# Pair DMAs behind dt's weights, an earlier split of the gated result, a state copy on VectorE and two transposes swapped, in a hybrid SSD and attention layer

## The chip, the cores and the metric

The kernel runs on one core of one Trainium2 chip. The metric is the device time in microseconds of one execution, the median over several runs; lower is better. The engines of the core are TensorE (PE in the profile, with PEld for its weight loads), VectorE (DVE), ScalarE (ACT), GpSimd (POOL) and SyncE (SP). Each engine works through its own queue in the order in which its instructions were queued. DMAs are issued from the queues of SP, ACT and POOL; in the profile's DMA tables SP's are q1, ACT's q10 and POOL's q0.

## The reference

One decoder layer (`DEPTH` 1) on 256 tokens of width 2048, in float32. Cut to what matters here:

```python
u = rmsnorm(h, norm_mix_pre)
proj = u @ w_in                       # z | x,B,C | dt | q | k | v
xbc = silu(causal_depthwise_conv(xbc, conv_w, conv_b))       # width 4
dt = softplus(dt_raw + dt_bias)                              # 32 heads
y = ssd_chunked(xh, dt, -exp(a_log), bm, cm)                 # chunks of 128 tokens
y = y + d_skip * xh
yg = y * silu(z)                                             # per group of 4 heads:
yg = yg * rsqrt(mean(yg * yg) + EPS)
y_ssm = yg * ssm_norm_w
y_att = dilated_attention(q, k, v)                           # three dilations, 16 heads
h = h + rmsnorm(concat(y_ssm, y_att) @ w_out, norm_mix_post)
h = h + rmsnorm(relu(rmsnorm(h, norm_mlp_pre) @ w_up) ** 2 @ w_down, norm_mlp_post)
```

In `ssd_chunked` the second chunk's output takes in a state that the first chunk leaves for each group: `states = B^T (decay * x dt)`, and `y_off = exp(a_cs) * (C @ state)`.

## The kernel before

**Precision and weights.** Each operand of a product is split into a high and a low part (`split`, lines 144 to 150): ScalarE writes the high part, VectorE the rest. Line 147 and 148 are the split without a scale, 149 and 150 the one with a scale. A block of weights is 256 rows by 512 columns, 512 KB. `fetch` (line 152) loads it from SP's queue into one of `RAWS` = 4 raw tiles, and `weights` (line 293) splits it into one of `BUFS` = 5 pairs of tiles `hi` and `lo`. So up to nine blocks are on their way ahead of PE. These instructions have the priority `AHEAD`, above all others.

**Who sets the order.** A planner goes through the program when it is built and fixes the order of every engine's queue: of the instructions that it holds to be ready, the one with the highest priority goes first, and priority falls with the place in the program. `tc.high_priority(offset=n)` moves the instructions in its block up by n places. In a block with `tc.manual_schedule()` the order of the text holds.

**Pairs.** Some blocks are multiplied with a scheme of seven products in place of eight (`seven`, line 377). It needs the sum of a block's second columns over its two row halves. `next_pair` (line 267) makes it in DRAM, from POOL's queue: a touch of the place (line 275: one column from an on-chip tile, only for the first use of each of the five places, so that the pair waits for that tile), a copy of the first rows (line 276) and an accumulating DMA of the second rows (line 277). `pair_of` (line 283) makes the next pair and hands out the one whose turn it is; the first to ask is the first z unit. Four pairs (`PAIRS_AHEAD`) are made ahead: the loop at lines 859 to 861 does so as soon as the last of the transposed input `u(NK - 1)` is there.

**The first stage.** `first_block` multiplies B's first 512 columns while the input is loaded and transposed. Then come C's block, X's block, the z unit (`gates`), another X block, and the same for the second half. A block of B, C or X runs in `gemm_features` (line 481): PE products at lines 475 and 478, eight steps of two input tiles. The evicted block goes through `conv` (lines 736 to 749): multiplied by the token scale into `pad` (740), whose three first columns POOL has set to zero (739), then four taps on ScalarE and VectorE (745, 747) and SiLU (749).

**Work between the steps.** After each step `pump` resumes one of the waiting generators. `steps` (line 653) is dt: it loads the 32 dt columns of `w_in` into `raw_dt` from ACT's queue (655; 2,048 rows of 128 bytes), splits them into `wdt` (657), and two resumptions later issues 32 matmuls (662, 663) in the middle of C's block. Then it computes softplus and the cumulative sums. `first_conv` (728) spreads the token scale `rstd` over the partitions (`over_partitions`, line 629: VectorE makes a diagonal, line 634, PE multiplies, line 635). `rstd` itself comes from POOL (line 142, a power), after VectorE's line 141.

**A group.** `ssd_group` (line 779) runs for each of eight groups of four heads. It forms C B^T, masks it (792), transposes B and x (790, 800), scales x by dt (805), makes the decays (816 to 818), and multiplies the first chunk's state (821). The state is copied to `st` (823) and multiplied by C (825); `yo` scales it (827). Line 833 multiplies within the chunks, 836 to 846 add, gate and normalise. Three resumptions later the result `yg` is transposed by PE (853) into one small PSUM tile, and split from there into `sh` and `sl` (854 to 856; the instructions have lines 149 and 150). The small PSUM tiles (`psmall`) have two banks.

**The end of the mix.** `mix_to_up` (line 1084) has its order written out. It finishes the last columns of the `w_out` product, adds the residual (`add`, 1121), transposes the sum (`turn`, 1131), splits it (`take`) and multiplies the first columns of `w_up` (`rows`). `turn` has three pairs of banks in rotation, which the table `turns` gives by its entries' order.

Of the kernel before, what the change touches and what calls it, by code (L numbers as in the profile page):

```python
# [10 lines left out]
F32 = mybir.dt.float32  # L11
F32R = mybir.dt.float32r
BF16 = mybir.dt.bfloat16
AF = mybir.ActivationFunctionType
# [3 lines left out]
S = 256  # L18
D = 2048
NT = S // P  # L20
NK = D // P
# [22 lines left out]
AHEAD = 1_000_000  # L44
# [11 lines left out]
PAIRS_AHEAD = 4  # L56
# [21 lines left out]
def hymba_layer(ctx: ExitStack, tc: tile.TileContext, x, norm_mix_pre, w_in, conv_w, conv_b, dt_bias, a_log,  # L78
                d_skip, ssm_norm_w, w_out, norm_mix_post, norm_mlp_pre, w_up, w_down, norm_mlp_post,
                consts, out):  # L80
    nc = tc.nc
# [21 lines left out]
    def u(k):  # L103

        t, i = us[k]
        return t[:, i]

    new_u()
    sh = big.tile([P, NK, S], F32R, name="sh")
    sl = big.tile([P, NK, S], F32R, name="sl")  # L110
# [21 lines left out]
    def bank():  # L132
        return pacc.tile([P, NB], F32, name="acc")

    def psmall():
        return psm.tile([P, NB], F32, name="ps")
# [7 lines left out]
    def split(hi, lo, src, scale=None):  # L144

        if scale is None:
            return (nc.scalar.activation(hi, src, AF.Copy),  # L147
                    nc.vector.tensor_tensor(lo, src, hi.bitcast(F32), op=ALU.subtract))  # L148
        return (nc.scalar.activation(hi, src, AF.Copy, scale=scale),
                nc.vector.scalar_tensor_tensor(lo, src, scale, hi.bitcast(F32), op0=ALU.mult, op1=ALU.subtract))  # L150
# [27 lines left out]
    room = {}  # L178
# [75 lines left out]
    pairs = []  # L254
# [12 lines left out]
    def next_pair():  # L267

        if not pairs:
            return  # L270
        src, ca, k = pairs.pop(0)
        cb = slice(ca + NB, ca + 2 * NB)
        d = places[len(paired) % len(places)]
        if len(paired) < len(places):
            nc.gpsimd.dma_start(d[:, 0:1], u(NK - 1)[:, 0, 0:1].bitcast(F32))
        nc.gpsimd.dma_start(d, src[k * KB * P:(k * KB + 1) * P, cb])
        nc.gpsimd.dma_start(d, src[(k * KB + 1) * P:(k * KB + 2) * P, cb], accum_op=ALU.add)
        paired.append((src, ca, k, d))
# [4 lines left out]
    def pair_of(src, ca, k):  # L283

        next_pair()
        s_, c_, k_, d = paired[turn_of["pair"]]
        assert (s_ is src) and (c_, k_) == (ca, k), (c_, k_, ca, k)
        turn_of["pair"] += 1
        return d
# [223 lines left out]
    w_pre, w_mlp, w_ssm, cb = par[:, 0:16], par[:, 16:32], par[:, 32:48], par[:, 48:80]  # L513
# [139 lines left out]
    def steps():  # L653
        raw = sp1.tile([P, NK, 32], F32, name="raw_dt")
        nc.scalar.dma_start(raw, w_in[:, COL_DT:COL_DT + 32].rearrange("(k p) n -> p k n", p=P))
        wdt = sp1.tile([P, NK, 64], F32R, name="wdt")
        split(wdt[:, :, 0:32], wdt[:, :, 32:64], raw)
        yield
        yield
        acc = psmall()  # L660
        for k in range(NK):
            nc.tensor.matmul(acc[:64, :S], wdt[:, k], u(k)[:, 0], start=k == 0, stop=False)
            nc.tensor.matmul(acc[:64, :S], wdt[:, k], u(k)[:, 1], start=False, stop=k == NK - 1)
        both = sp1.tile([64, S], F32, name="both")
        nc.vector.tensor_copy(both, acc[:64, :S])
        yield
        p = psmall()
        for t in range(NT):
            nc.tensor.matmul(p[:, t * 32:(t + 1) * 32], both[:, t * P:(t + 1) * P], two[:64], start=True, stop=True)
        with tc.high_priority(offset=AHEAD):  # L670
            y = sp1.tile([P, NT, 32], F32, name="dt_y")
            for t in range(NT):
                nc.vector.scalar_tensor_tensor(y[:, t], p[:, t * 32:(t + 1) * 32], rstd[:, t:t + 1], bias_b,
                                               op0=ALU.mult, op1=ALU.add)

            e = sp1.tile([P, NT, 32], F32, name="dt_e")
            nc.vector.scalar_tensor_tensor(e, y, -1.0, y, op0=ALU.mult, op1=ALU.min)
            nc.scalar.activation(e, e, AF.Exp)
            r = sp1.tile([P, NT, 32], F32, name="dt_r")
            nc.vector.tensor_scalar(r, e, 2.0, None, op0=ALU.add)  # L680
            nc.vector.reciprocal(r, r)
            s = sp1.tile([P, NT, 32], F32, name="dt_s")
            nc.vector.tensor_mul(s, e, r)
            q = sp1.tile([P, NT, 32], F32, name="dt_q")
            nc.vector.tensor_mul(q, s, s)
            h = sp1.tile([P, NT, 32], F32, name="dt_h")
            nc.vector.tensor_scalar(h, q, 2.0 / 17, None, op0=ALU.mult)
            for n in (15, 13, 11, 9, 7, 5, 3):
                nc.vector.scalar_tensor_tensor(h, h, 2.0 / n, q, op0=ALU.add, op1=ALU.mult)
            nc.vector.scalar_tensor_tensor(h, h, 2.0, s, op0=ALU.add, op1=ALU.mult)  # L690
            nc.vector.scalar_tensor_tensor(dt, y, 0.0, h, op0=ALU.max, op1=ALU.add)
            ea = sp1.tile([P, 32], F32, name="dt_a")
            nc.scalar.activation(ea, a_b, AF.Exp)
        yield
        with tc.high_priority(offset=AHEAD):
            for t in range(NT):
                nc.vector.scalar_tensor_tensor(dA[:, t], dt[:, t], -1.0, ea, op0=ALU.mult, op1=ALU.mult)
        for _ in range(7):
            yield
        p = psmall()  # L700
        for t in range(NT):
            nc.tensor.matmul(p[:, t * 32:(t + 1) * 32], triu, dA[:, t], start=True, stop=True)
        nc.tensor.matmul(p[:, 64:96], ones, dA[:, 0], start=True, stop=True)
        nc.vector.tensor_copy(acs.rearrange("p t h -> p (t h)"), p[:, 0:64])
        nc.scalar.activation(eacs, acs[:, 1], AF.Exp)
        nc.vector.tensor_sub(toend, p[:, 64:96], acs[:, 0])
        nc.scalar.activation(toend, toend, AF.Exp)
        p = psmall()
        for t in range(NT):
            nc.tensor.matmul(p[:32, t * P:(t + 1) * P], dA[:, t], triu, start=True, stop=True)  # L710
        rowed = sp1.tile([32, S], F32, name="rowed")
        nc.vector.tensor_copy(rowed, p[:32, :S])
        nc.scalar.dma_start(acs_d, rowed)
# [65 lines left out]
    def ssd_group(sp, g, bT, cT, xT, z):  # L779
# [6 lines left out]
        p = psmall()  # L786
# [10 lines left out]
        p = psmall().rearrange("p (c f) -> p c f", c=NT)  # L797
# [22 lines left out]
        p = psmall()  # L820
        nc.tensor.matmul(p[:, :S], bn, xdd.rearrange("p r d -> p (r d)"), start=True, stop=True)
        st = sp.tile([P, HPG * HD], F32, name="st")
        nc.scalar.activation(st, p[:, :S], AF.Copy)
        yield
        nc.tensor.matmul(p[:, S:], cT[:, P:], st, start=True, stop=True)
        yo = sp.tile([P, HPG, HD], F32, name="yo")
# [3 lines left out]
        p = psmall().rearrange("p (c r d) -> p c r d", c=NT, r=HPG)  # L830
# [19 lines left out]
        p = psmall().rearrange("p (f s) -> p f s", f=2)  # L850
        for f in range(2):
            for c in range(NT):
                nc.tensor.transpose(p[:, f, c * P:(c + 1) * P], yg[:, c, f * P:(f + 1) * P], ident)
        for f in range(2):
            k = 2 * g + f
            split(sh[:, k], sl[:, k], p[:, f], w_ssm[:, k:k + 1])

    sp = ssd.enter_context(tc.tile_pool(name="sp", bufs=2, side="right", reuse_waits="tile"))
    with tc.high_priority(offset=AHEAD):
        for _ in range(PAIRS_AHEAD):  # L860
            next_pair()
    zs = []
    for hb in range(2):
        bT = conv_block(COL_B + hb * NB, 16 + 4 * hb, first if hb == 0 else None)
# [3 lines left out]
        for xb in (2 * hb, 2 * hb + 1):  # L868
# [3 lines left out]
            for j in range(2):  # L872
                g = 2 * xb + j
# [181 lines left out]
    def columns(n):  # L1055
        return slice(n * NB, (n + 1) * NB)
# [27 lines left out]
    def mix_to_up(c0, ks, acc):  # L1084


        up = [bank() for _ in range(NT)]
        banks, turned = {}, {}
        turns = [(0, 0), (0, 1), (1, 0), (0, 2), (1, 1), (1, 2), (1, 3), (0, 3)]
        weighed = hp.tile([P, NT, NB], F32, name="e")  # L1090
        room_w = big.tile([P, SUMS, 2, S], F32R, name="ua").rearrange("p k b s -> p k (b s)")

# [26 lines left out]
        def add(t, n):  # L1119
            cs = columns(n)  # L1120
            nc.vector.scalar_tensor_tensor(of_h(t, cs), weighed[:, t] if n == 3 else mw_at(t, cs), rm[:, t:t + 1],
                                           of_h(t, cs), op0=ALU.mult, op1=ALU.add)

        def turn(t, n):
            at = turns.index((t, n)) % 3
            if at not in banks:
                banks[at] = [bank() if banks else psmall() for _ in range(2)]
            p = turned[t, n] = banks[at]
            for f in range(4):
                k = 4 * n + f  # L1130
                nc.tensor.transpose(p[f % 2][:, f // 2 * P:(f // 2 + 1) * P], of_h(t, slice(k * P, (k + 1) * P)), ident)
# [7 lines left out]
        def square(t, n):  # L1139
            junk = hp.tile([P, NB], F32, name="junk")  # L1140
            nc.scalar.activation(junk, of_h(t, columns(n)), AF.Square, accum_out=ssh[:, t, n:n + 1])

        o, w = {}, {}
        with tc.high_priority(offset=AHEAD), tc.manual_schedule():
# [47 lines left out]
            rows(0, 2)  # L1192
            add(1, 1)
            square(1, 0)
            turn(0, 2)
            turn(1, 0)
            take(1, 0)
            rows(0, 3)
            take(0, 4)
# [63 lines left out]
    def of_h(t, cs):  # L1263

        i, c0 = divmod(cs.start, 3 * NB)
        return hs[i][:, t, c0:c0 + cs.stop - cs.start]
# [234 lines left out]
```

## Time and profile before

| | |
|---|---|
| median of 3 runs | 1470.46 us (1469.34 to 1471.87) |
| the profiled execution | 1471.31 us |
| its span, first to last instruction | 1469.3 us |
| mean granted PE clock | 0.995 |
| DMA | 328.25 MB, mean 223 GB/s |
| packets of POOL's queue (q0) | 17,632, 40.91 MB |
| packets of ACT's queue (q10) | 7,872, 13.68 MB |

All times within the profile are microseconds from the start of the span. A timeline row has the start, the length, the engine, the line, the operation and its tiles (output `<-` inputs); in brackets stands how long the engine was idle before it and what released it. Rows with the engine SPq, ACTq or POOLq belong to that engine's queue of DMA issues. A wait row names the waiting engine, tile and line, what it waited for, and the time in total, the number of waits and the longest. A row of a stretch has its length and then, for PE, PEld, DVE, ACT and POOL, the busy time and in brackets the count of instructions; then the granted clock of PE (1.00 is full), the DMA share and GB/s. A queue row has packets, MB and the share of the 16 DMA engines' time.

### The profile page before, as it was taken

The page shows a single profiled execution, that of the slowest core. Times are in us where ns is not written, and L with a number is a line of the kernel's source. Part 1 is how long each engine was busy: PE and PEld are TensorE (multiplying, and loading weights), DVE is VectorE, ACT ScalarE, POOL GpSimd, SP SyncE. Part 2 cuts the span into 40 slices and gives each one's busy share as a digit, 9 for nine tenths or more (in the row PEclk, how much of TensorE's full clock was granted, in tenths as well). Part 3 has the DMA queues.
Part 4 walks back from the last instruction along what each step waited for, and adds up shares of the span by engine and source line. Part 5 has one row for each costly group of instructions (what it writes and reads, how often), then busy time and mean ns, then how long its engine had stood idle before and what let it go on. Part 6 is the DMA issues. An engine that isn't in the chain of part 4 may idle for free.

```text
span 1469.3 us, 20379 instructions
## 1 busy us (share of the span) xinstructions
PE 1450.1 (99%) x7099; PEld 1223.3 (83%) x7099; DVE 1277.6 (87%) x1835; ACT 938.4 (64%) x1352; POOL 149.7 (10%) x226
## 2 busy tenths in 40 slices
PE   9899999999999999999999999999999999999998
PEld 8788888888888888888888888888888888888886
DVE  7498888988998587579888999999879999999997
ACT  7378669657566566556557676666555766765664
POOL 1101220022010010001100011001111111101000
PEclk9999999999999999999999999999999999999999
DMA  8868656765685577588876798778888888789854
GB/s 263 231 197 226 196 167 181 225 199 147 213 254 165 141 214 216 187 256 257 261 240 190 210 320 250 200 214 253 247 240 280 244 251 256 215 270 270 252 179 160
DMA packets 170199, 328.25 MB, mean 223 GB/s; under 512 B 15616, under 2 KB 18544, under 8 KB 170096
## 3 DMA queue, kind: packets, MB, share of 16 engines
q1 hardware_dynamic: 144592, 272.37, 57.7%
q0 software_dynamic: 17632, 40.91, 13.9%
q10 hardware_dynamic: 7872, 13.68, 2.8%
q8 instruction: 55, 0.90, 0.2%
q14 instruction: 48, 0.39, 0.1%
HBM read 322.67 MB, written 45.12 MB: 250 GB/s over the span
## 4 chain that ended last, share of the span: by engine, by line
PE 84%; DVE 1%; ACT 0%; issue 0%; POOL 0%; DVEq 0%; ACTq 0%
PE acc L330 11%; PE acc L329 11%; PE acc L328 11%; PE acc L475 9%; PE acc L411 6%; PE acc L413 6%; PE acc L412 6%; PE acc L478 5%; PE ps L328 3%; PE ps L330 3%; PE ps L329 3%; PE ps L411 2%; PE ps L413 2%; PE ps L412 2%; PE ps L833 1%; PE acc L1408 1%
## 5 line engine op out<-in xcount | busy, mean ns | idle before, releaser
L148 DVE TENSOR_TENSOR lo<-raw,hi 128x1024 fp32r<-128x1024 f32 (+1 forms) x392 | 475.3, 1218 | 92.6 <-ACT hi L147 88.2
L147 ACT ACTIVATE hi<-raw 128x1024 fp32r<-128x1024 f32 (+1 forms) x392 | 409.6, 1050 | 206.0 <-PE acc L330 70.7
L475 PE MATMUL acc<-ua,hi 128*128 128x512 f32 x600 | 162.9, 400 | 0.0
L475 PEld LDWEIGHTS acc<-ua,hi 128*128 128x128 f32 x600 | 105.8, 190 | 16.3
L147 ACT ACTIVATE hi<-e 128x1024 fp32r<-128x1024 f32 x64 | 68.0, 1063 | 71.1 <-DVE e L252 66.0
L478 PEld LDWEIGHTS acc<-ua,lo 128*128 128x128 f32 x600 | 88.1, 190 | 10.0
L478 PE MATMUL acc<-ua,lo 128*128 128x256 f32 x600 | 91.1, 282 | 0.0
L328 PE MATMUL acc<-hi,sh 128*128 128x512 f32 x224 | 88.4, 395 | 0.0
L330 PE MATMUL acc<-hi,sl 128*128 128x512 f32 x224 | 87.3, 390 | 0.0
L329 PE MATMUL acc<-lo,sh 128*128 128x512 f32 x224 | 87.2, 389 | 0.0
L328 PE MATMUL acc<-hi,ua 128*128 128x512 f32 x216 | 85.5, 396 | 0.0
L329 PE MATMUL acc<-lo,ua 128*128 128x512 f32 x216 | 84.3, 390 | 0.2 <-DVE lo L148 0.2
L330 PE MATMUL acc<-hi,ua 128*128 128x512 f32 x216 | 84.3, 390 | 0.0
L148 DVE TENSOR_TENSOR lo<-e,hi 128x1024 fp32r<-128x1024 f32 x64 | 77.9, 1217 | 0.0
L475 PE MATMUL acc<-uc,hi 128*128 128x512 f32 x240 | 69.8, 402 | 0.0
L412 PE MATMUL acc<-lo,ah 128*128 128x512 f32 x174 | 67.8, 389 | 0.0
L411 PE MATMUL acc<-hi,ah 128*128 128x512 f32 x174 | 67.8, 389 | 0.0
L413 PE MATMUL acc<-hi,al 128*128 128x512 f32 x174 | 67.7, 389 | 0.0
L148 DVE TENSOR_TENSOR lo<-ha,hi 128x1024 fp32r<-128x1024 f32 x43 | 52.3, 1219 | 5.9 <-ACT hi L147 5.7
L147 ACT ACTIVATE hi<-ha 128x1024 fp32r<-128x1024 f32 x43 | 45.2, 1056 | 17.1 <-PE acc L330 9.8
L147 ACT ACTIVATE hi<-r 128x512 fp32r<-128x512 f32 x64 | 40.2, 627 | 18.2 <-PE acc L330 7.1
L330 PE MATMUL acc<-hi,al 128*128 128x512 f32 x128 | 49.8, 389 | 0.0
(544 smaller groups left out, 3616.8 us busy)
## 6 DMA issues: line engine op xcount, KB each, us to landing
raw<-in_w_in_dram SPq DMA_DIRECT2D x161, 512.0 KB, 4.3
raw<-in_w_down_dram SPq DMA_DIRECT2D x72, 512.0 KB, 5.4
raw<-in_w_up_dram SPq DMA_DIRECT2D x65, 512.0 KB, 4.6
raw<-in_w_out_dram SPq DMA_DIRECT2D x38, 512.0 KB, 5.4
pair<-in_w_up_dram POOLq DMA_DIRECT2D x56, 256.0 KB, 5.3
raw<-pair SPq DMA_DIRECT2D x52, 256.0 KB, 4.4
pair<-in_w_down_dram POOLq DMA_DIRECT2D x50, 256.0 KB, 6.1
ha<-in_w_up_dram SPq DMA_DIRECT2D x20, 512.0 KB, 5.0
```

Source lines behind the costliest of these rows:

```text
L147: return (nc.scalar.activation(hi, src, AF.Copy), nc.vector.tensor_tensor(lo, src, hi.bitcast(F32), op=ALU.subtract))
L148: nc.vector.tensor_tensor(lo, src, hi.bitcast(F32), op=ALU.subtract))
L328: nc.tensor.matmul(dst, a_h[:, r, ts], hi[:, j], start=begin and j == 0, stop=False)
L329: nc.tensor.matmul(dst, a_h[:, r, ts], lo[:, j], start=False, stop=False)
L330: product[t] = nc.tensor.matmul(dst, a_l[:, r, ts], hi[:, j], start=False, stop=end and j == KB - 1)
L411: nc.tensor.matmul(dst, a_h, hi[:, j], start=own and first, stop=False)
L412: nc.tensor.matmul(dst, a_h, lo[:, j], start=False, stop=False)
L413: nc.tensor.matmul(dst, a_l, hi[:, j], start=False, stop=own and last)
L475: nc.tensor.matmul(acc[f], hi[:, j, f * P:(f + 1) * P], u(k0 + j), start=k0 + j == 0, stop=False, skip_group_check=True)
L478: nc.tensor.matmul(acc[f][:, 0], lo[:, j, f * P:(f + 1) * P], u(k0 + j)[:, 0], start=False, stop=k0 + j == NK - 1, skip_group_check=True)
L833: nc.tensor.matmul(p[:, c, r], bc[:, r, c * P:(c + 1) * P], xdt[:, c, r], start=True, stop=True)
L1408: nc.tensor.transpose(p[:, f * P:(f + 1) * P], r[:, f * P:(f + 1) * P], ident)
```

## The change

Four edits:

1. The loop that makes the first four pairs moves from ahead of the blocks into `steps`, behind the split of dt's weights, and the touch of a place now reads a column of the low half of `wdt` in place of a column of `u(NK - 1)`.
2. The copy of the group's state runs on VectorE in place of ScalarE.
3. The split of a group's transposed result gets a priority 200 places higher.
4. In `mix_to_up`, `turn(1, 0)` and `turn(0, 2)` change places. The banks are now handed out in the order of the calls, which gives each call the banks that it had.

```diff
@@ next_pair
         if len(paired) < len(places):
-            nc.gpsimd.dma_start(d[:, 0:1], u(NK - 1)[:, 0, 0:1].bitcast(F32))
+            nc.gpsimd.dma_start(d[:, 0:1], room["pairs"])
@@ steps
         wdt = sp1.tile([P, NK, 64], F32R, name="wdt")
         split(wdt[:, :, 0:32], wdt[:, :, 32:64], raw)
+        room["pairs"] = wdt[:, 0, 32:33].bitcast(F32)
+        with tc.high_priority(offset=AHEAD):
+            for _ in range(PAIRS_AHEAD):
+                next_pair()
         yield
@@ ssd_group
-        nc.scalar.activation(st, p[:, :S], AF.Copy)
+        nc.vector.tensor_copy(st, p[:, :S])
...
-        for f in range(2):
-            k = 2 * g + f
-            split(sh[:, k], sl[:, k], p[:, f], w_ssm[:, k:k + 1])
+        with tc.high_priority(offset=200):
+            for f in range(2):
+                k = 2 * g + f
+                split(sh[:, k], sl[:, k], p[:, f], w_ssm[:, k:k + 1])
 
     sp = ssd.enter_context(tc.tile_pool(name="sp", bufs=2, side="right", reuse_waits="tile"))
-    with tc.high_priority(offset=AHEAD):
-        for _ in range(PAIRS_AHEAD):
-            next_pair()
@@ mix_to_up
-        banks, turned = {}, {}
-        turns = [(0, 0), (0, 1), (1, 0), (0, 2), (1, 1), (1, 2), (1, 3), (0, 3)]
+        banks, turned = [], {}
...
-            at = turns.index((t, n)) % 3
-            if at not in banks:
-                banks[at] = [bank() if banks else psmall() for _ in range(2)]
-            p = turned[t, n] = banks[at]
+            if len(banks) < 3:
+                banks.append([bank() if banks else psmall() for _ in range(2)])
+            p = turned[t, n] = banks[len(turned) % 3]
...
+            turn(1, 0)
             turn(0, 2)
-            turn(1, 0)
             take(1, 0)
```

## The prediction

> **What bounds the kernel now.** First the page's head and its busy times, then the waits of TensorE (PE), then the stretches around each long wait.
>
> ```profile
> span 1469.3 us, 20379 instructions
> PE 1450.1 (99%) x7099; PEld 1223.3 (83%) x7099; DVE 1277.6 (87%) x1835; ACT 938.4 (64%) x1352; POOL 149.7 (10%) x226
> ```
>
> PE is the bound: only work that it no longer does, or time in which it no longer stands still, moves the end. The change removes no matmul, so all depends on its waits. The two longest inside the kernel (engine, tile and line; releaser; us in total, times, longest):
>
> ```profile
> PE ps L662 <- DVE wdt L148: 7.1, 1, 7.1
> PE ps L821 <- DVE sl L150: 2.6, 1, 2.6
> ```
>
> The first is dt's projection waiting for its split weights; the timeline around it, first column the start and second the length:
>
> ```profile
> 37.47 0.39 ACTq L655 DMA_DIRECT2D raw_dt<-in_w_in_dram  x1
> ...
> 47.93 2.00 PE L475 MATMUL acc<-ub,hi 128*128 128x512 f32 x8
> ...
> 49.77 1.11 PE L478 MATMUL acc<-ub,lo 128*128 128x256 f32 x8
> ...
> 56.56 0.63 ACT L147 ACTIVATE wdt<-raw_dt 128x512 fp32r<-128x512 f32 x1 [9.16 <-DMA raw_dt<-in_w_in_dram]
> ...
> 57.22 0.69 DVE L148 TENSOR_TENSOR wdt<-raw_dt,wdt 128x512 fp32r<-128x512 f32 x1 [8.57 <-ACT wdt L147]
> 57.97 0.47 PE L662 MATMUL ps<-ua,wdt 128*64 128x256 f32 x1 [7.09 <-DVE wdt L148]
> ```
>
> PE runs out at 50.88 (49.77 + 1.11). The load was issued at 37.47, and the split follows its landing at once: the load is late, nothing else. Why it is late is in the DMA queues. First the load's time to landing, then packets and MB in the stretches 41 to 51, 53 to 54 and 54 to 55 us:
>
> ```profile
> DMA to landing us min/median/max: 19.1/19.1/19.1
> ```
>
> ```profile
> q0 software_dynamic: 585, 1.13, 57.4%
> q1 hardware_dynamic: 836, 1.62, 46.0%
> q10 hardware_dynamic: 839, 0.11, 7.0%
> ```
>
> ```profile
> q1 hardware_dynamic: 185, 0.36, 93.8%
> q10 hardware_dynamic: 183, 0.02, 14.9%
> ```
>
> ```profile
> q1 hardware_dynamic: 122, 0.22, 58.0%
> q10 hardware_dynamic: 444, 0.06, 35.9%
> ```
>
> q0 carries POOL's pair DMAs, q1 SP's weight blocks, q10 dt's weights: 2,048 rows of 128 bytes. q10 gets one packet for each of q1's. While the pairs run that is 84 a us (839 in 10 us); with the weight blocks alone 183; with q1 partly idle 444.
>
> Each long wait has a second price. Stretches: us; PE busy; granted clock after POOL's column.
>
> ```profile
> 57.97:62.90 4.93, 4.93 (x23) 4.93 (x24) 4.73 (x7) 3.01 (x4) 0.00 (x0) 0.50 0.45 127
> ...
> 208.47:213.10 4.63, 4.62 (x15) 3.72 (x16) 3.42 (x6) 0.81 (x3) 0.73 (x1) 0.63 0.77 246
> ```
>
> Behind the first wait PE works 4.93 us at half clock and loses about half of it, 2.3 us; behind the second 4.63 x 0.37 = 1.7 us. So the waits cost 7.09 + 2.3 = 9.4 us and 2.65 + 1.7 = 4.3 us.
>
> [...]
>
> **The pairs behind dt's weights.** Fifteen POOL DMAs (a touch, a copy and an accumulation for each of five pairs: four from the moved loop, the fifth from the first `pair_of`, whose touch reads the same place) now cannot begin before VectorE's half of the dt split is written. Rows: POOL's queue and its neighbours, in order.
>
> ```profile
> 30.44 2.89 POOL L275 DMA_DIRECT2D pair<-uc  x5 [29.99 <-ACT uc L149]
> ...
> 39.96 0.17 DVE L141 TENSOR_SCALAR rm<-sq 128x2 f32<-128x2 f32 x1
> ...
> 44.71 1.07 POOL L142 TENSOR_TENSOR rstd<-rm,half 128x2 f32<-128x2 f32 x1
> ...
> 53.93 0.88 POOL L277 DMA_DIRECT2D pair<-in_w_in_dram  x1 [8.15 <-DMA pair<-in_w_in_dram]
> ...
> 66.77 0.61 PE L635 MATMUL ps<-dg,ones 128*128 128x128 f32 x4
> ...
> 99.78 0.34 SPq L156 DMA_DIRECT2D raw<-pair  x1
> ```
>
> With q0 silent, how soon do dt's weights land? At most four raw blocks (RAWS) wait unsplit ahead of the wdt split on ScalarE; at 512 KB in 2 KB rows these are 1,024 packets. Beside them q10 moves 1,024 rows at 183 a us, 5.6 us, and the other 1,024 at 444, 2.3 us: from 41 to 48.9, and some 0.3 us to land. With the two halves of the split (0.63 + 0.69) and 0.1 us between them, PE may start at about 50.7, against 50.88. Bounds: SP's queue never pauses, 2,048 / 183 = 11.2 us, start 54.0, a wait of 3.1 us and its clock of about 1.7; or no wait at all. I take 0.3 us, by the row with q1 partly idle, as four buffers cannot keep SP busy. Gain 9.4 - 0.3 = **9.1 us**, with 4.6 and 9.4 as ends.
>
> What the moved DMAs meet: they now run from about 51 to 75 us. Their chain took 24.4 us (30.44 to 54.81) and the first pair is read at 99.78, some 90 after the gain, so they keep 15 us. SP then has q0 beside it: 84 packets a us against the 87 that PE consumes (256 in the 2.95 us from 47.93 to 50.88), with four blocks already fetched. Nothing is lost while they last. On POOL a pad's memset can stand behind the fifth pair's accumulation; the convolution behind it has no reader for tens of us, but VectorE's weight splits queue behind that convolution. They run five blocks ahead of PE, 14 us, which covers it.
>
> **The gated result's split first.** Timeline, PE's transposes, VectorE's queue and PE's wait:
>
> ```profile
> 193.89 0.60 PE L853 MATMUL ps<-ident,yg 128*128 128x128 f32 x4
> ...
> 201.63 3.25 DVE L747 SCALAR_TENSOR_TENSOR cT<-pad,cw,cT 128x256 f32<-128x256 f32 x8
> ...
> 204.80 0.47 DVE L150 SCALAR_TENSOR_TENSOR sl<-ps,par,sh 128x256 fp32r<-128x256 f32 x1
> ...
> 207.86 0.86 DVE L150 SCALAR_TENSOR_TENSOR sl<-ps,par,sh 128x256 fp32r<-128x256 f32 x2
> ...
> 208.47 0.67 PE L821 MATMUL ps<-xdd,bn 128*128 128x256 f32 x2 [2.65 <-DVE sl L150]
> ```
>
> The transposed tile holds one of two small PSUM banks from 194.5 until VectorE has split it, at 208.3, behind the convolutions (L747); L821 needs the bank. Ahead of them, four splits of 0.47 us fit on VectorE before 201, even behind two weight splits, and PE wants the bank at 205.8. The convolutions come 1.9 us later, and their rows are read only in the next half's groups. Gain **4.3 us**; ends 0 (L821 then waits for something else) and 4.3.
>
> **The state copy on VectorE.** ScalarE's row (ns minimum, median, maximum), then a like copy on VectorE, then PE's use of the state and VectorE's next step in the last two groups:
>
> ```profile
> L823 ACT ACTIVATE st<-ps x8: 361/384/424, 154.9 to 349.5; 128x256 f32<-128x256 f32 x8
> ```
>
> ```profile
> 68.25 0.42 DVE L636 COPY rbc<-ps 128x256 f32<-128x256 f32 x1
> ...
> 347.94 0.60 PE L825 MATMUL ps<-st,cT 128*128 128x256 f32 x2
> ...
> 351.58 0.75 DVE L827 TENSOR_TENSOR yo<-ps,eacs 128x256 f32<-128x256 f32 x2
> ```
>
> 0.42 for 0.38 us is nothing; the queue matters. A VectorE that runs late makes PE wait at L825. Here it reached the next step 3.0 us after L825 ended (351.58 against 348.54). Ends: a gain of 0.2 us (ScalarE freed), a loss of 3.0 + 1.7 us of clock at one pair of groups. The groups' splits leave VectorE's queue earlier here as well, so I take 0.4 us of loss.
>
> **The swapped transposes in the mix's end.**
>
> ```profile
> 785.07 0.75 DVE L1121 SCALAR_TENSOR_TENSOR ha<-mw,rmix,ha 128x512 f32<-128x512 f32 x1
> ...
> 785.49 0.60 PE L1131 MATMUL ps<-ident,ha 128*128 128x128 f32 x4
> ...
> 785.92 0.61 PE L1131 MATMUL acc<-ident,ha 128*128 128x128 f32 x4
> ...
> 787.01 0.50 PE L329 MATMUL acc<-lo,ua 128*128 128x512 f32 x1 [0.25 <-DVE lo L148]
> ```
>
> The banks stay as they were; only the order of two fours turns. Token tile 1's now goes first and must await the sum that ends at 785.82, so PE stands 0.43 us; of this 0.25 us is idle already, at 787.01. Cost 0.2 us; ends 0 and 0.4.
>
> **Sum.** 9.1 + 4.3 - 0.4 - 0.2 = 12.8 us: the profiled span goes from 1469.3 to 1456.5. That execution took 1471.31 us, 2.0 around the span; the median of three, 1470.46, is the base: **1457.7 us**.
>
> **Rivals.** (a) *dt's weights still late* (3.1 + 1.7 us, the bound above): 1462.2. For it: 183 a us would never do; against: four buffers. (b) *PE waits for the state copy, or L821 for another releaser*, 4.3 to 4.7 us back: 1462. For it: VectorE's 87% and its lateness at 351.58; against: seven other groups had more room. (c) *Slower: rstd behind the pairs.* POOL runs in order, and in the profile rstd's power (44.71) stands behind fourteen of the fifteen pair DMAs. If it is queued behind all of them, it comes 24.4 us after the first touch at 50.8: at 75.2, done 76.3, and L635 at 76.9 instead of 66.77. That is 10.1 us and about 2 of clock, less 4.3: 1478.3. Behind fourteen again it would be 14.3 us (44.71 - 30.44), L635 about where it is, 2 us of clock, less 4.3: 1468.2. It decides from the moment rstd is queued behind any accumulation. Against: its input is ready at 40.1 (39.96 + 0.17), while the wdt split is three splits further on in VectorE's queue. (d) *It doesn't do what it says*: waits stay, 1470.
>
> **How the numbers follow.** Forecast 0.61, (a) 0.13, (b) 0.13, (c) 0.05 behind all and 0.03 behind fourteen, (d) 0.05. A change under 0.2% (2.9 us) can't be told from none. So faster is forecast, (a) and (b), 0.87; within are (d) and the milder (c), 0.08; slower is (c) behind all, 0.05. The forecast alone: 1456.5 to 1460 (all terms at their good ends give 1470.46 - 9.4 - 4.3 - 0.2 = 1456.6, and a run strays by 1 us). With (a) and (b) the range is **1455.8 to 1464.5**.
>
> **What would show it.** The pairs' first touch stands behind the wdt split, and dt's weights land within 12 us of issue; L662 follows the matmuls at 50.9 with less than 0.5 us of wait and the clock stays at 1.00 there; rstd comes before 46. In the group stage L821 has no wait on a split, the clock row stays at 1.00, and st on VectorE has no waiter on PE. A landing after 15 us, a PE wait over 2 us anywhere before 400 us, or rstd behind the touches would make it wrong.

## The result and the profile after

| | before | after |
|---|---|---|
| median | 1470.33 us (1469.28 to 1471.87, 6 runs) | 1459.28 us (1458.31 to 1462.32, 6 runs) |
| the profiled execution, its span | 1471.31 us, 1469.3 us | 1459.04 us, 1457.3 us |
| mean granted PE clock | 0.995 | 0.999 |

The ratio is 0.9927 with a 95% interval of 0.9914 to 0.9939: 11 us faster. The page's head and busy times of the changed kernel:

```profile
span 1457.3 us, 20381 instructions
PE 1446.1 (99%) x7099; PEld 1219.4 (84%) x7099; DVE 1281.2 (88%) x1843; ACT 939.1 (64%) x1346; POOL 150.3 (10%) x226
```

PE has the same 7,099 matmuls and is 4.0 us less busy (1450.1 before), which fits the half clock that the prediction put behind the two waits (2.3 and 1.7 us). The other 8 us of the span's 12.0 are idle time that is gone. TensorE's waits (engine, tile, line; releaser; us in total, times, longest):

```profile
PE ps L825 <- DVE sl L150: 1.8, 1, 1.8
...
PE ps L837 <- DVE yo L831: 0.7, 1, 0.7
```

The wait on dt's weights, 7.1 us before, is gone from the list. The wait on the group's split is not: 2.6 us at L821 has become 1.8 at L825, which is the same matmul (edit 1 adds four lines above it). The timeline around dt, start and length first:

```profile
36.08 0.39 ACTq L655 DMA_DIRECT2D raw_dt<-in_w_in_dram  x1
...
38.81 0.72 POOL L142 TENSOR_TENSOR rstd<-rm,half 128x2 f32<-128x2 f32 x1 [2.45 <-DVE rm L141]
...
43.12 0.63 ACT L147 ACTIVATE wdt<-raw_dt 128x512 fp32r<-128x512 f32 x1 [1.55 <-DMA raw_dt<-in_w_in_dram]
...
43.78 0.69 DVE L148 TENSOR_TENSOR wdt<-raw_dt,wdt 128x512 fp32r<-128x512 f32 x1 [0.95 <-ACT wdt L147]
...
44.80 2.91 POOL L275 DMA_DIRECT2D pair<-wdt  x5 [5.26 <-DVE wdt L148]
...
48.35 1.11 PE L478 MATMUL acc<-ub,lo 128*128 128x256 f32 x8
49.30 0.28 PE L666 MATMUL ps<-ua,wdt 128*64 128x256 f32 x1
```

```profile
DMA to landing us min/median/max: 7.0/7.0/7.0
```

The load lands 7.0 us after its issue (19.1 before), both halves of the split are written by 44.5, and the first dt matmul overlaps the modelled end of the one before it. The pairs' touches come after the split, and `rstd` goes ahead of them at 38.81. Behind dt PE comes to L635:

```profile
55.90 0.61 PE L635 MATMUL ps<-dg,ones 128*128 128x128 f32 x4
```

That is 10.87 us earlier than before (66.77). But 1.42 of these were there before dt: the last products ahead of it began at 48.35, against 49.77. The profiled execution of before lost this time in its first 9 us, ahead of all that the edits touch; among it is a wait of 0.6 us on its input (L556) that the changed kernel's execution does not have. So between the two executions the dt stage gave 9.45 us, and 1.42 of the span's 12.0 are not the change's.

The stretch that ran at 0.50 before now has the full clock (us; PE, PEld, DVE, ACT, POOL busy; clock; DMA share; GB/s):

```profile
49.20:56.10 6.90, 6.90 (x53) 6.55 (x52) 1.64 (x2) 1.36 (x2) 2.78 (x4) 1.00 1.02 364
```

And dt's queue, first in the stretch from 39 to 50 us, then in its first microsecond:

```profile
q1 hardware_dynamic: 1477, 2.84, 81.5%
q10 hardware_dynamic: 1969, 0.25, 14.7%
q0 software_dynamic: 126, 0.00, 0.8%
...
q10 hardware_dynamic: 1418, 0.18, 115.2%
q1 hardware_dynamic: 36, 0.05, 15.5%
```

While SP's queue is nearly empty, q10 moves 1,418 rows in one microsecond, against 839 in ten beside both other queues before. In the group stage, the second four transposes before, and then the changed kernel:

```profile
197.10 0.60 PE L853 MATMUL ps<-ident,yg 128*128 128x128 f32 x4
```

```profile
186.63 0.60 PE L857 MATMUL ps<-ident,yg 128*128 128x128 f32 x4
...
188.83 0.47 DVE L150 SCALAR_TENSOR_TENSOR sl<-ps,par,sh 128x256 fp32r<-128x256 f32 x1
...
191.15 0.86 DVE L150 SCALAR_TENSOR_TENSOR sl<-ps,par,sh 128x256 fp32r<-128x256 f32 x2
191.77 0.67 PE L825 MATMUL ps<-xdd,bn 128*128 128x256 f32 x2 [1.76 <-DVE sl L150]
```

The split does go ahead of the convolutions, as edit 3 says. But PE now asks for the bank at 190.01 (191.77 - 1.76), 3.4 us after the second four transposes began at 186.63. Before, it asked at 205.82 (208.47 - 2.65), and its second four began at 197.10: 8.7 us. The planner moved the matmul up as well: counted in the traces, it stands 20 matmuls behind the first of these transposes, against 50 before.

### The profile page after: what moved, and what is told of

Its sections match the earlier page's. It is cut to its first block, busy times and chain, and to the rows that moved or that the text cites. A ratio compares the mean times of both kernels' runs of the same rounds, so it can differ in the third digit from the quotient of the medians.

```text
span 1457.3 us, 20381 instructions
## 1 busy us (share of the span) xinstructions
PE 1446.1 (99%) x7099; PEld 1219.4 (84%) x7099; DVE 1281.2 (88%) x1843; ACT 939.1 (64%) x1346; POOL 150.3 (10%) x226
## 4 chain that ended last, share of the span: by engine, by line
PE 95%; DVE 3%; ACT 1%; issue 1%; POOL 0%; ACTq 0%; DVEq 0%
PE acc L475 13%; PE acc L328 11%; PE acc L330 11%; PE acc L329 11%; PE acc L478 7%; PE acc L412 6%; PE acc L413 6%; PE acc L411 6%; PE ps L330 3%; PE ps L328 3%; PE ps L329 3%; PE ps L412 3%; PE ps L413 2%; PE ps L411 2%; DVE lo L148 1%; PE ps L837 1%
## 5 line engine op out<-in xcount | busy, mean ns | idle before, releaser
L329 PE MATMUL acc<-lo,sh 128*128 128x512 f32 x224 | 87.2, 389 | 0.0
L329 PE MATMUL acc<-lo,ua 128*128 128x512 f32 x216 | 84.2, 390 | 0.0
```

The costliest lines, as they stand in the source:

```text
L329: nc.tensor.matmul(dst, a_h[:, r, ts], lo[:, j], start=False, stop=False)
```

## The experiments

The theory after the result: edit 1 is the whole gain, because only the dt stage's two prices (wait and half clock) have gone. The main rival: edit 3 carries part of it, as forecast. Others: edits 2 and 4 give something back.

**Each edit alone.** Pairs only:

```diff
+        room["pairs"] = wdt[:, 0, 32:33].bitcast(F32)
+        with tc.high_priority(offset=AHEAD):
+            for _ in range(PAIRS_AHEAD):
+                next_pair()
...
-    with tc.high_priority(offset=AHEAD):
-        for _ in range(PAIRS_AHEAD):
-            next_pair()
```

> Only the pairs' loop and its touch are moved behind dt's weights; all else as before. Theory (the two queues beside dt's weights made them late): they land 7 us after issue as in the changed kernel instead of 19, the 7.1 us wait at the dt matmuls and the half clock behind it go, and the time falls by 9.0 to 9.6 us, to about 1461; the 2.65 us wait on the gated result's split stays. Rival (the changed kernel's gain of 11 us comes from its other edits, or from rstd being earlier in POOL's queue): below 6 us.

Split only:

```diff
-        for f in range(2):
+        with tc.high_priority(offset=200):
+            for f in range(2):
```

> Only the split of the gated result has its higher priority. Theory: the bank is free earlier, but PE's next user of it (the state's matmul) also moves up in PE's queue, by more than two steps of the block, so a wait of 1 to 2 us on the same split stays and only the clock's share (1.7 us) and 0.5 to 1 us are gained: 2 to 3 us, to about 1468. Rival, as predicted: the wait goes entirely, 4.3 us, 1466. The dt wait of 7.1 us stays in both.

State copy only:

```diff
-        nc.scalar.activation(st, p[:, :S], AF.Copy)
+        nc.vector.tensor_copy(st, p[:, :S])
```

> Only the state copy goes to VectorE. Theory: it gains nothing by itself; with the state's matmul and its reader next to each other in PE's queue PE waits for VectorE at one or two of the four pairs of groups: 0 to 2 us slower. Rival (ScalarE freed helps): 0.5 us or more faster.

Swap only:

```diff
-            turn(0, 2)
             turn(1, 0)
+            turn(0, 2)
```

> Only the two calls of turn change places; the banks are the same. Theory: PE stands 0.4 us at the transposes and regains 0.25 us at the next weights: 0 to 0.4 us slower, within the noise of the time; in the trace a wait of some 0.2 us at the transposes takes the place of the wait of 0.25 us at line 329. Rival: over 1 us either way.

| | median, us | ratio to before (95%) |
|---|---|---|
| before, beside them | 1470.25 (25 runs) | |
| pairs only | 1458.84 (1458.24 to 1459.09, 4 runs) | 0.992 (0.9905 to 0.9934) |
| split only | 1469.34 (1466.93 to 1472.29, 10 runs) | 0.9995 (0.9985 to 1.0005) |
| state copy only | 1470.7 (1468.95 to 1471.68, 10 runs) | 1.0001 (0.9992 to 1.001) |
| swap only | 1469.27 (1468.51 to 1472.84, 10 runs) | 0.9992 (0.9983 to 1.0001) |

Pairs only gains 11.4 us (9.7 to 14.0 by its interval), all that the change gains; the other three cannot be told from no change. Two expectations missed in size: 9.0 to 9.6 us for the pairs, and 2 to 3 us for the split, which gave 0.9 with an interval that holds none. Pairs only, the group stage in the timeline and then the stretch behind the wait:

```profile
186.26 0.60 PE L857 MATMUL ps<-ident,yg 128*128 128x128 f32 x4
...
193.96 0.47 DVE L150 SCALAR_TENSOR_TENSOR sl<-ps,par,sh 128x256 fp32r<-128x256 f32 x1
...
197.02 0.86 DVE L150 SCALAR_TENSOR_TENSOR sl<-ps,par,sh 128x256 fp32r<-128x256 f32 x2
...
197.63 0.67 PE L825 MATMUL ps<-xdd,bn 128*128 128x256 f32 x2 [2.65 <-DVE sl L150]
```

```profile
197.63:203.00 5.37, 5.37 (x34) 4.73 (x34) 3.40 (x6) 2.15 (x5) 0.73 (x1) 1.00 0.79 257
```

The group's wait is as long as before, yet the clock behind it stays at 1.00: this run lost 2.65 us there, not 4.3. Put beside the changed kernel, edit 3 brought the first VectorE split from 7.7 us behind the transposes (193.96 - 186.26) to 2.2 (188.83 - 186.63), and PE's request from 8.7 behind them to 3.4. The two shifts nearly cancel. It is edit 3 that moves the matmul: with the split at its higher priority it stands 20 matmuls behind the transposes (the change in both its profiles, split only, highest priority), and 50 in every profile with the old priority (before, pairs only, state copy only, swap only and three more below), where no resumption was moved. Split only shows the same wait, in a list that keeps dt's:

```profile
PE ps L662 <- DVE wdt L148: 7.7, 1, 7.7
PE ps L821 <- DVE sl L150: 1.7, 1, 1.7
```

State copy only and then swap only, the stretch behind the wait of 2.6 us at L821:

```profile
208.20:213.00 4.80, 4.80 (x16) 3.97 (x17) 3.39 (x6) 1.48 (x3) 0.00 (x0) 0.65 0.77 245
```

```profile
207.69:213.00 5.31, 5.31 (x33) 4.68 (x34) 3.40 (x6) 2.14 (x5) 0.73 (x1) 1.00 0.83 262
```

One lost clock, the other did not, though neither edit touches that wait. Swap only also shows the dt stage of a run that came to it at 49.45, without the late start of before's profile; the first row is PE's wait, the second the stretch behind it:

```profile
49.45:57.31 7.86, 0.01 (x2) 0.01 (x1) 0.69 (x1) 1.41 (x2) 0.88 (x1) 0.69 0.78 195
57.31:62.90 5.59, 5.59 (x27) 5.59 (x28) 5.09 (x7) 3.01 (x4) 0.00 (x0) 0.52 0.76 206
```

That is 7.86 us and 5.59 x 0.48 = 2.7 us of clock, 10.5 in all. Swap only and pairs only both kept their clock in the group stage, and their spans differ by 10.0 (1467.1 and 1457.1). The wait of swap only at the mix's end, and that of the changed kernel:

```profile
PE acc L1131 <- DVE ha L1121: 0.2, 1, 0.2
```

```profile
773.74 0.66 PE L1131 MATMUL acc<-ident,ha 128*128 128x128 f32 x4 [0.23 <-DVE ha L1122]
```

The swap puts a wait of 0.23 us in the place of the 0.25 us at L329.

**Is it the pairs' traffic?** Two tests of dose. In the first, two pairs early, two of the four moved pairs stay at their old place, and the other two go behind the split:

```diff
-            for _ in range(PAIRS_AHEAD):
+            for _ in range(PAIRS_AHEAD - 2):
                 next_pair()
...
+    room["pairs"] = u(NK - 1)[:, 0, 0:1].bitcast(F32)
+    with tc.high_priority(offset=AHEAD):
+        for _ in range(2):
+            next_pair()
```

> As the kernel with the pairs' move alone, but two of the four pairs begin at the old place and two behind dt's weights. Theory (dt's weights share the DMA engines with POOL's and SP's queues in turns): with half of the pair traffic ahead of them they land between the two ends, 10 to 16 us after issue (7 with none, 19 with four), and PE waits 0 to 4 us at the dt matmuls; time 1459 to 1465. Rival (what counts is only whether any pair stands ahead of rstd in POOL's queue): 19 us and the wait of 7 us as before.

One run gave 1465.39 us. PE's wait, then the queues from 41 to 51 us, then the load's time to landing:

```profile
PE ps L666 <- DVE wdt L148: 3.6, 1, 3.6
```

```profile
q1 hardware_dynamic: 1023, 1.96, 53.6%
q0 software_dynamic: 288, 0.52, 28.5%
q10 hardware_dynamic: 779, 0.10, 6.9%
```

```profile
DMA to landing us min/median/max: 15.6/15.6/15.6
```

Half of POOL's packets in that window (288 for 585) leave a landing of 15.6 us and half of the wait. Both lie where the theory had them, and the rival's 19 us and 7 us did not come; the time is 0.4 us above the theory's.

The second, copies alone, takes the kernel before and leaves out the accumulations of the first five pairs, so that only touches and copies run early:

```diff
-        nc.gpsimd.dma_start(d, src[(k * KB + 1) * P:(k * KB + 2) * P, cb], accum_op=ALU.add)
+        if len(paired) >= len(places):
+            nc.gpsimd.dma_start(d, src[(k * KB + 1) * P:(k * KB + 2) * P, cb], accum_op=ALU.add)
```

> As before, with the pairs at their old place, but the accumulating DMAs of the first five pairs are left out (the copies and touches stay), so that the second halves of these sums are missing. Theory: the copies are nearly done when the first rows of dt's weights move; the accumulations, of 2 KB a packet at 176 ns, are what they wait behind. They land within 11 us of issue and PE does not wait over 1 us. Rival: the copies hold SP's blocks back, so that these stand beside dt's weights, which still land after 14 us or more.

One run gave 1461.19 us. The landing, the queues from 41 to 51, and PE at dt:

```profile
DMA to landing us min/median/max: 12.1/12.1/12.1
```

```profile
q1 hardware_dynamic: 1317, 2.53, 71.3%
q10 hardware_dynamic: 2031, 0.26, 16.5%
q0 software_dynamic: 78, 0.23, 5.7%
```

```profile
48.21 1.11 PE L479 MATMUL acc<-ub,lo 128*128 128x256 f32 x8
49.44 0.33 PE L663 MATMUL ps<-ua,wdt 128*64 128x256 f32 x1
```

Without the accumulations q0 has 78 packets in the window, for 585 before, and PE has no wait at dt, though the pairs are still made ahead of it. The landing is 1.1 us later than expected, but early enough. So it was the accumulations, the later half of the pairs' chain, that dt's weights were held up beside. Whether by their number or by their price a packet, these two runs do not separate.

**What is edit 3 worth in the whole change?** Once the change without it, and once with the highest priority in place of 200:

```diff
-        with tc.high_priority(offset=200):
-            for f in range(2):
+        for f in range(2):
```

> The changed kernel with the gated result's split back at its old priority (the pairs' move, the state copy and the swap stay). Theory (in the changed kernel the split shortens PE's wait from 2.65 to 1.76 us, and what it gains goes back at line 837): within 1 us of the changed kernel's 1459.3; the wait on the split is 2.6 us again. Rival, as predicted: 4 us slower, 1463.

```diff
-        with tc.high_priority(offset=200):
+        with tc.high_priority(offset=AHEAD):
```

> The changed kernel with the split's priority above all others (AHEAD in place of 200). PE's order in the first half's groups stays. Theory (the split waits behind pads and weight splits that the planner holds to be ready sooner, not behind priorities): the wait on it at the state's matmul stays at 1.2 to 2 us and the time is within 1 us of the changed kernel's. Rival: the wait goes and the time falls by 1.5 us or more.

Beside a before of 1469.94 us (9 runs), the change without edit 3 took 1460.87 us (1459.15 to 1463.3, 5 runs; ratio 0.9935, 0.9922 to 0.9947), the one with the highest priority 1459.5 (1458.79 to 1463.44, 5 runs; 0.9926, 0.9912 to 0.9939). These intervals and the change's own overlap. The first is 1.6 us above the change's median, where at most 1 was expected, and far from the rival's 4; the noise does not tell 1.6 from nothing. Without edit 3, the wait and the stretch from its start:

```profile
PE ps L825 <- DVE sl L150: 2.6, 1, 2.6
```

```profile
194.91:200.00 5.09, 2.45 (x12) 2.14 (x13) 4.94 (x8) 1.88 (x3) 0.10 (x1) 1.00 0.63 194
```

With the highest priority, the longest of PE's waits and a stretch that begins 0.8 us behind its end:

```profile
PE ps L829 <- DVE st L827: 1.8, 1, 1.8
```

```profile
201.60:205.00 3.40, 3.40 (x11) 2.72 (x10) 2.53 (x5) 0.56 (x2) 0.72 (x1) 0.50 0.60 171
```

No wait on the split is left in its list, and one on the state copy has taken its place: behind the convolutions, VectorE now reaches `st` late. The theory had the wait on the split stay, and that was wrong; the time is within 1 us of the change's, as it said, because one wait replaced another. That is the second rival of the prediction, in this variant alone; in the change itself the wait on `st` is 0.2 us.

**A version without the wait.** If PE asks too early, the matmul of the state can come one step later, with one empty step fewer ahead of the transposes, so that the generator has as many steps as before:

```diff
+        yield
         p = psmall()
         nc.tensor.matmul(p[:, :S], bn, xdd.rearrange("p r d -> p (r d)"), start=True, stop=True)
...
-        yield
         p = psmall().rearrange("p (f s) -> p f s", f=2)
```

In the changed kernel, with the changed kernel itself run again beside it:

> The changed kernel, with the state's matmul one resumption later in each group and one resumption fewer ahead of the transposes. Theory (the wait of 1.8 us on the split is left only because the matmul moved up in PE's queue): it comes two steps later, the wait on the split and the 0.7 us wait at line 837 go, and the time is 1.5 to 2.5 us below the changed kernel's. Rival: the wait moves to another releaser (the state copy on VectorE, yo) and the time is within 0.5 us of the changed kernel's, or above it.

> The changed kernel once more, on the same chip as the others of this batch, to compare them by more runs: 1458.5 to 1460. With the pairs' move alone at 1458.8 the other three edits give together between 0.5 us less and 1 us more.

And with edit 1 alone:

> The pairs' move, and the state's matmul one resumption later, without the other three edits. Theory (the split's priority and the later matmul are both needed): the split ends near 197.6 in the kernel with the pairs' move alone, and the matmul then stands near 195, so a wait of 1.5 to 3 us on the split stays: 1457.5 to 1460. Rival (the later place is enough): no wait on the split and 1456 to 1457, as with all edits.

| | median, us | ratio to before (95%) |
|---|---|---|
| the change again | 1459.26 (1458.38 to 1461.32, 6 runs) | 0.9925 (0.9912 to 0.9938) |
| the change, state later | 1456.65 (1456.09 to 1457.62, 4 runs) | 0.9909 (0.9894 to 0.9923) |
| edit 1, state later | 1458.16 (1457.46 to 1458.47, 4 runs) | 0.9916 (0.9903 to 0.993) |

The first two ran on the same chip beside the same runs of before (1469.83 us, 11 runs), and their runs do not overlap (1458.38 at least, 1457.62 at most): 2.6 us between the medians, slightly more than expected. Timeline of the change with the state later, splits and first matmul of the state:

```profile
186.39 0.60 PE L857 MATMUL ps<-ident,yg 128*128 128x128 f32 x4
...
189.86 0.86 DVE L150 SCALAR_TENSOR_TENSOR sl<-ps,par,sh 128x256 fp32r<-128x256 f32 x2
...
195.20 0.59 PE L826 MATMUL ps<-xdd,bn 128*128 128x256 f32 x2
```

The matmul of the state now starts 8.8 us behind the last transposes (195.20 - 186.39) and waits for nothing; at `yo` 0.4 us of wait is left, where none was expected. With edit 1 and the later state, but the split at its old priority, part of the wait stays:

```profile
PE ps L826 <- DVE sl L150: 1.2, 2, 0.9
```

So the early split takes a wait away once PE does not move up with it. The times of the two alone do not show it: they ran on different chips, their ratios' intervals overlap, and edits 2 and 4 differ too. The version with all four edits and the later state was the fastest that ran.

## Why the prediction was right, and where it was not

- **The sum.** 12.8 us were forecast and 11.05 measured in the medians (9.0 to 12.6 by the interval); the time of 1459.28 lies within the range, 1.6 us above the point.
- **dt's weights, 9.1 us: right in mechanism, under-sized.** In the two profiled executions the stage gave 9.45 us, the forecast's 9.4 with no wait left. (One reading in it is off: 4.93 us at 0.50 lose 2.5 us, not 2.3.) Edit 1 alone gave 11.4 in the medians, and 10.0 between two profiled runs that are alike elsewhere. The step that was short is the wait and its clock, taken from one execution with a late start: PE ran out there at 50.88, against 49.45 in swap only, while the wait ended only 0.66 us later (57.97 against 57.31). So that execution waited 7.09 us, where swap only waited 7.86 and paid 2.7 of clock. 10.0 and 10.5 lie within the interval of the 11.4; 9.1 does not. The rest is not settled. A clock that edit 1's runs kept in the group stage would fit: all four read a mean clock of 0.999, as does their profile, which lost none there, while six of the 25 runs of before read 0.994, as does the profile of state copy only, which lost it.
- **The landing.** By the prediction's rows PE could start at 50.7, before its need at 50.88, and it allowed 0.3 us of wait all the same. The split came 4.8 us ahead of need: VectorE had the split ready at 44.5 and PE came at 49.3. The estimate gave q10 444 rows a microsecond at best, the highest row of before; with only 36 packets of q1 beside it, it moved 1,418. The sum lost only the 0.3. Rival (a) falls with it.
- **The group's split, 4.3 us: the failed step.** "PE wants the bank at 205.8" was taken as fixed when the split moved. It was not: L825 moved up 30 matmuls, 5.3 us, against the transposes, in every kernel with edit 3 and in none without, as long as no resumption was moved. Why the planner does so is not shown; that a bank which is released earlier makes its next user ready earlier would fit. What was left is 0.9 us of wait (2.65 to 1.76). The other 1.7 us, the clock, was priced as sure. After waits of 2.6 us it was lost in before, state copy only and both tests of dose, and kept in pairs only, swap only and the change without edit 3.
- **State copy, -0.4 us, and swap, -0.2.** Alone, neither can be told from nothing, and that is within the bounds. VectorE did come late at `yo` with both edits in (0.7 us at L837 for 0.3 before, and 1.4 in the profile of the change run again), which is of the size of the 0.4 forecast, at another line. Neither edit does it alone: the change without edit 3 has 0.3 there, split only 0.4 and state copy only 0.4. With both it comes in the change, but not at the highest priority. The swap exchanged one wait for another.
- **The other rivals.** `rstd` came at 38.81, ahead of all touches: (c) did not happen, for the reason given. (b) did not happen in the change: its wait on `st` is 0.2 us, and L825 waits for the same split as before. With the split at the highest priority it did, at 1.8 us.
- **The marks.** Landing under 12 us, no wait at L666 (as L662 is called now), full clock there and an early `rstd` all held, and so did the full clock in the group stage, as it happens. "L821 has no wait on a split" did not, nor quite "no waiter" on `st` (0.2 us).

The forecast landed that near the time by luck: a term too small by one or two microseconds stood beside one too large by about three.

## What to carry to other kernels

A small load of short rows that is issued while a long chain of background transfers runs is the one to protect: here the chain began 14 us later (44.80 for 30.44) without being missed, and making its first transfer depend on the small load's split was worth 11 us by the medians of edit 1 alone. A planner that orders all queues does not hold the rest still when one priority is raised: before pricing a wait as removed, ask whether the waiter will be moved up too, and if it is, move the waiter down. A half-clock penalty seen behind one wait in one execution is a possible cost of that wait, not a part of every run's.

## What the hardware showed unexpectedly

**The clock behind a wait.** Waits of 2.6 us on the same split were followed by a clock of 0.63 (before), 0.65 (state copy only) and 0.69 (copies alone), but by 1.00 in pairs only, swap only and the change without edit 3. In two pairs early, with the same wait, the clock was 0.79 from 199 to 205 us, which holds the wait, and 0.92 from 205 to 210. With the split at the highest priority a wait of 1.77 us ended at 200.79, and the clock was 1.00 up to 201.60 and 0.50 from there to 205.00. Behind one of 1.76 in the changed kernel it stayed at 1.00:

```profile
191.78:196.00 4.22, 4.22 (x23) 3.69 (x24) 4.22 (x10) 4.19 (x6) 0.10 (x1) 1.00 0.60 153
```

So the length of a wait does not decide alone. Nor did the clock fall at the wait's end, but 0.8 us behind it with the highest priority and 1.2 us behind it in before (209.68 for 208.47). In before it fell three times, at 56.08, 209.68 and 1465.78 us, and came back after 6.83 us, after 3.41, and not before the end of the span. In this execution the first two falls lie 153.60 us apart and the last two 1256.11, which is 45 and 368 times 3.413. The 3.41 us ahead of the second fall hold the wait for the split:

```profile
206.27:209.68 3.41, 1.21 (x6) 1.10 (x7) 3.25 (x7) 1.77 (x4) 0.10 (x1) 1.00 0.61 176
```

PE was idle for 2.2 us of them (3.41 - 1.21), and ran at half clock for the next 3.41, to 213.09. Why one wait of 2.6 us was followed by half clock and another was not, no run shows.

**Packets of unlike price.** In the stretch from 41 to 51 us of before, a packet of POOL's queue (1.13 MB in 585, 1.9 KB each) held a DMA engine for 157 ns (57.4% of 16 engines for 10 us, over 585), one of SP's (1.62 MB in 836, also 1.9 KB) for 88 ns (46.0%, over 836). By single records it is the accumulations: in that stretch their 2 KB packets took 176 ns at the median, SP's 2 KB packets 98, and the 4 KB packets of the pairs' copies 159. From 46 to 50 us POOL's queue got 271 packets, SP's 269 and ACT's 271, so dt's rows of 128 bytes advanced only as fast as the long packets beside them. The three shares add up to 110%, so the records overlap in part, and the 157 and 88 ns are not exclusive time.
